# The tiles that epilogues read are requested on GpSimd's queue instead of SyncE's

## The chip, the cores and the metric

The kernel runs on one core of a Trainium2 chip. The metric is device time in microseconds (us), the time of one execution of the whole program. Five engines work side by side, each through its own list of instructions in order: TensorE (PE in the profile; PEld is its weight load), VectorE (DVE), ScalarE (ACT), GpSimd (POOL) and SyncE (SP), which here only issues transfers. A transfer is asked for by an instruction in the list of one of these engines ("a queue" below) and then runs on the core's 16 DMA engines. An engine that has to wait for a semaphore holds back everything behind that instruction in its own list.

## The reference

One layer of a hybrid decoder over 2,048 tokens (16 meta tokens ahead of them) of width 1,024, in float32. Cut to what matters here:

```python
u = rmsnorm(hres, norm_w)
proj = einsum('bld,dn->bln', u, w_in)          # inputs of both branches, and the merge gates
z, xbc, dt_raw, q, k, v, g_gla, a_lr, merge_g = split_cols(proj, IN_WIDTHS)
y_ssd, y_gla = ...                             # the two branches (Mamba-2 SSD, gated linear attention)
branches = stack([y_ssd, y_gla], axis=2)
branch_proj = einsum('blnc,ncd->blnd', branches, w_branch)
gates = sigmoid(merge_g.reshape(b, l, 2, 1024))
merged = sum(gates * branch_proj, axis=2)
h = hres + einsum('bld,de->ble', merged, w_out)
return rmsnorm(h, final_norm_w)[:, 16:]
```

Five matrix products of 2,048 x 1,024 x 1,024 are done in the part of the kernel that the change touches: the two merge gates, the two branch projections and the output projection.

## The kernel before

The kernel has two parts. The first (up to some 1,486 us) does the input projection and both branches; the change does not touch it. The second part does the five products named above, each split over two halves of the tokens where the stage is a gate or a branch. Its stages run one after the other: gate0, br00, br10 (first half of the tokens), gate1, br01, br11 (second half), out. Names in the trace: `g` are the gates in DRAM, `m` the merged rows, `out_h` the result, `in_xm` the residual rows, `in_w_br`, `in_w_o` and `in_w_feat` weights.

**Products.** Each stage multiplies blocks by a Strassen-like scheme with seven products in place of eight. A pair n has seven products p = 1 to 7; a product is 12 matmuls (four slices, three passes L211, L212, L213, since each float32 operand is split into a high and a low part) into a PSUM bank of 128 x 512. Products go in groups of 14, two pairs n and n+1 interleaved, in the order p = 1, 2, 6, 7, 5, 3, 4, each p first for n and then for n+1. There are 280 products in all; gate stages have 56, branch stages 28 each, the out stage 56. Three PSUM pools serve them: `psa` (three banks; p = 1, 6, 5 add into one bank, and p = 3 adds to it again), `psc` (p = 2) and `psb` (p = 7, 4). After p = 1, 6 and 5 ScalarE copies the bank to SBUF (`sn`, L1097, a snapshot), and p = 3 may add to the bank only when the snapshot that follows p = 5 has been taken.

**Operands.** For each product, SP loads the raw tiles: `load_b` (L1051, `br`, 256 KB, 28 for a stage, from a pool of five buffers and another of two) and `load_a` (L1063, `ar`, 256 KB, eight for each two pairs, from a pool of eight). ScalarE rounds the raw tile (L1056 for b, L1080 for a), VectorE makes the remainder (L1057, L1081); VectorE also adds a-tiles (L1071 to L1074).

**Epilogues.** A finished result is used by `use`. Gate stages take tanh on ScalarE (L1116) and store to `g`. Branch stages read the gate tile back (`fetch`, L1129, into an `io` buffer), multiply it with the result on VectorE (L1135), and the merged tile is stored to `m` for the first branch (L1031) and added into `m` by an accumulating transfer for the second (L1034). The out stage reads residual rows (`fetch`, L1152), adds half the snapshot and half the result (L1157, L1166), takes the sum of squares on ScalarE (L1172), raises it to the power -0.5 on GpSimd (L1182, a tile of 128 x 1), scales (L1187) and stores (L1031). All of these tiles come from one pool of eight `io` buffers; a buffer is free again when the store of what it held has landed.

**What sets the order.** The lists of PE and SP are in the order in which the program writes them: positions in units of a product, such as "three products ahead of its use" for a `fetch`, and "4.8 products ahead of its preparation" for a b-tile. Stores are issued on GpSimd. The lists of DVE, ACT and POOL are put in order by a scheduler from its own estimate of when each instruction becomes ready.

Each request of a queue reports its landing on one of eight counters, which are handed out in turn; a request therefore waits until the one eight places ahead of it in its own list has landed.

Of the kernel before, what the change touches and what calls it, by code (L numbers as in the profile page):

```python
# [14 lines left out]
P = 128  # L15
D = 1024
KT = 8
META = 16
BLK = 512
# [22 lines left out]
def trunk_kernel(ctx: ExitStack, tc: tile.TileContext, xm, xmt, w_feat, w_tok, w_zm, w_br, w_o,  # L42
                 cf32, cmsk, pvec, fnw, hvec, gw2, out):
    nc = tc.nc
# [20 lines left out]
    def left(name):  # L65
        return wdram.tile([P, BLK], F32, tag=name, name=name, bufs=1)
# [52 lines left out]
    for s in range(nsb):  # L119
        b = 2 * s + 2  # L120
# [898 lines left out]
    g_left = [[left(f"g_{b}_{i}") for i in range(16)] for b in range(nblk)]  # L1019
# [83 lines left out]
    def io():  # L1103
        return mk(opl, [P, BLK], F32, "io", bufs=8)

    def total(ps, snap):
        if snap is None:
            return ps
        nc.vector.tensor_tensor(snap, snap, ps, op=ALU.add)
        return snap  # L1110
# [12 lines left out]
    def branch_stage(s, nb):  # L1123
        got = {}

        def fetch(n, i, t):
            d, b = 2 * n + i, 2 * s + t
            got[n, i, t] = io()
            nc.sync.dma_start(got[n, i, t], g_left[b][nb * 8 + d])  # L1129

        def use(n, i, t, ps, snap):
            d, b = 2 * n + i, 2 * s + t
            th = got.pop((n, i, t))
            x = total(ps, snap)
            nc.vector.scalar_tensor_tensor(th, th, 1.0, x, op0=ALU.add, op1=ALU.mult)  # L1135
            if nb == 0:
                store(m_left[b][d // 4][:, d % 4], th)
            else:
                added.setdefault(step_no[0] + 2, []).append((m_left[b][d // 4][:, d % 4], th))

        return Stage(f"br{nb}{s}", ("b", nb, s), 4,
                     lambda n, i, j: w_br[nb * 8 + 2 * n + i, :, j * BLK:(j + 1) * BLK].rearrange(
                         "p (k c) -> p k c", c=P), use, fetch, 3)

    def out_stage():
# [3 lines left out]
        def fetch(n, i, t):  # L1149
            r0 = (2 * n + i) * P  # L1150
            res[n, i, t] = r = io()
            nc.sync.dma_start(r, xm[META + r0:META + r0 + P, t * BLK:(t + 1) * BLK])  # L1152

        def before(n, i, t, snap):
            r = res[n, i, t]
# [8 lines left out]
        def finish(row, n, i, t, ps):  # L1164
# [18 lines left out]
            for hf in (1 - t, t):  # L1183
# [11 lines left out]
                else:  # L1195
# [3 lines left out]
        return Stage("out", ("o",), seq // (2 * P),  # L1199
                     lambda n, i, j: m_left[(2 * n + i) // 4][j][:, :, (2 * n + i) % 4 * P:((2 * n + i) % 4 + 1) * P],  # L1200
                     use, fetch, 3, before)

    stages = []
# [150 lines left out]
```

## Time and profile before

| what | value |
|---|---|
| median of three runs | 2272.17 us (2272.05 to 2272.39) |
| the profiled execution | 2275.24 us, span 2273.5 us |
| mean granted clock of TensorE | 0.995 |
| busy share of the span: PE, DVE, ACT, POOL | 98%, 72%, 49%, 22% |
| `L1129` requests on SP (gate tiles) | 64 of 256 KB, 1635.2 to 2095.7 us |
| `L1152` requests on SP (residual rows) | 32 of 256 KB, 2098.5 to 2238.5 us |
| `L1031` and `L1034` requests on POOL | 184 of 256 KB, 1511.0 to 2232.7 us |

The profiled execution is 3.07 us longer than the median, and 1.74 us of it lie outside the span. Times in the views are microseconds from the start of the span. A row of the timeline gives start, length, engine, line, operation, the tile written and the tile read, and in square brackets the idle time of the engine just before and what ended it. In the table of stretches the columns are the stretch and its length, then busy time and number of instructions of PE, PEld, DVE, ACT and POOL, the granted clock, the DMA engines' share and GB/s. The second part takes the span from 1,486 us to its end; the br11 stage begins its products near 2,022 us and the out stage near 2,101 us.

### The profile page before, as it was taken

The page shows a single profiled execution, that of the slowest core. Times are in us where ns is not written, and L with a number is a line of the kernel's source. Part 1 is how long each engine was busy: PE and PEld are TensorE (multiplying, and loading weights), DVE is VectorE, ACT ScalarE, POOL GpSimd, SP SyncE. Part 2 cuts the span into 40 slices and gives each one's busy share as a digit, 9 for nine tenths or more (in the row PEclk, how much of TensorE's full clock was granted, in tenths as well). Part 3 has the DMA queues.
Part 4 walks back from the last instruction along what each step waited for, and adds up shares of the span by engine and source line. Part 5 has one row for each costly group of instructions (what it writes and reads, how often), then busy time and mean ns, then how long its engine had stood idle before and what let it go on. Part 6 is the DMA issues. An engine that isn't in the chain of part 4 may idle for free.

```text
span 2273.5 us, 36613 instructions
## 1 busy us (share of the span) xinstructions
PE 2232.8 (98%) x12699; PEld 1950.6 (86%) x12699; DVE 1629.2 (72%) x3323; ACT 1123.6 (49%) x2510; POOL 499.0 (22%) x633
## 2 busy tenths in 40 slices
PE   9899999999999999999999999999999999999998
PEld 9899888888888989888988898878888888887786
DVE  5787866687775578676579755785778866787876
ACT  5555555454444454443455343464644545554443
POOL 3344533122321222222122200012111122111211
PEclk9999999999999999999999999999999999999999
DMA  8767865667886666886576655475769865779653
GB/s 267 236 212 242 299 219 205 215 189 236 268 281 201 202 224 209 272 275 222 186 229 218 222 182 167 151 239 183 264 217 288 244 210 198 273 269 242 195 165 111
DMA packets 282377, 507.50 MB, mean 223 GB/s; under 512 B 27104, under 2 KB 134880, under 8 KB 282192
## 3 DMA queue, kind: packets, MB, share of 16 engines
q1 hardware_dynamic: 218096, 415.33, 55.7%
q0 software_dynamic: 16928, 48.77, 7.0%
q10 hardware_dynamic: 47168, 41.07, 5.5%
q8 instruction: 99, 1.62, 0.3%
q14 instruction: 86, 0.70, 0.1%
HBM read 357.87 MB, written 147.19 MB: 222 GB/s over the span
## 4 chain that ended last, share of the span: by engine, by line
PE 72%; DVE 9%; issue 9%; DMA 5%; ACT 3%; POOL 2%; SPq 1%; ACTq 0%; POOLq 0%; DVEq 0%
PE pj L211 13%; PE pj L213 13%; PE pj L212 13%; PE psa L211 4%; PE psa L213 4%; PE psa L212 4%; PE psb L213 2%; PE psb L211 2%; PE psb L212 2%; PE pc L653 2%; PE pc L823 2%; PE pc L654 1%; PE pc L923 1%; PE psc L213 1%; PE psc L211 1%
## 5 line engine op out<-in xcount | busy, mean ns | idle before, releaser
L211 PE MATMUL pj<-u,whl 128*128 128x512 f32 (+1 forms) x1184 | 445.9, 377 | 9.6 <-ACT acc L563 5.2
L213 PE MATMUL pj<-u,whl 128*128 128x512 f32 (+1 forms) x1184 | 429.9, 363 | 0.0
L212 PE MATMUL pj<-u,whl 128*128 128x512 f32 (+1 forms) x1184 | 429.1, 362 | 0.0
L211 PE MATMUL pj<-whl,u 128*128 128x256 f32 (+1 forms) x992 | 288.3, 291 | 0.9 <-DMA whl<-k_zm 0.5
L213 PE MATMUL pj<-whl,u 128*128 128x256 f32 (+1 forms) x992 | 281.5, 284 | 0.6 <-DVE u L284 0.6
L212 PE MATMUL pj<-whl,u 128*128 128x256 f32 (+1 forms) x992 | 281.4, 284 | 0.0
L211 PEld LDWEIGHTS pj<-u,whl 128*128 128x128 f32 x1184 | 224.0, 189 | 47.6 <-ACT acc L563 6.2
L211 PE MATMUL psa<-b,a 128*128 128x512 f32 x640 | 250.0, 391 | 5.1 <-ACT sn L1097 5.1
L213 PEld LDWEIGHTS pj<-u,whl 128*128 128x128 f32 x1184 | 223.7, 189 | 35.6
L212 PEld LDWEIGHTS pj<-u,whl 128*128 128x128 f32 x1184 | 224.3, 189 | 33.0
L213 PE MATMUL psa<-b,a 128*128 128x512 f32 x640 | 249.3, 389 | 0.7 <-DVE a L1081 0.7
L212 PE MATMUL psa<-b,a 128*128 128x512 f32 x640 | 249.0, 389 | 0.0
L211 PEld LDWEIGHTS pj<-whl,u 128*128 128x128 f32 x992 | 189.3, 191 | 2.9 <-DMA whl<-k_zm 1.4
L213 PEld LDWEIGHTS pj<-whl,u 128*128 128x128 f32 x992 | 189.2, 191 | 1.0 <-DVE u L284 1.0
L212 PEld LDWEIGHTS pj<-whl,u 128*128 128x128 f32 x992 | 189.3, 191 | 0.4
L193 POOL TENSOR_TENSOR whl<-wr,whl 128x512 fp32r<-128x512 f32 (+1 forms) x96 | 135.8, 1423 | 170.3 <-ACT whl L190 134.3
L567 DVE SCALAR_TENSOR_TENSOR acc<-cin,hcw,acc 128x512 f32<-128x512 f32 (+1 forms) x192 | 160.1, 834 | 15.0 <-ACT acc L563 12.8
L1081 DVE TENSOR_TENSOR a<-ar,a 128x512 fp32r<-128x512 f32 x160 | 110.1, 688 | 78.2 <-ACT a L1080 77.6
L85 POOL TENSOR_TENSOR wr<-wr 128x256 f32<-128x256 f32 x80 | 68.8, 860 | 418.1 <-DMA wr<-u 163.1
L1056 ACT ACTIVATE b<-br 128x512 fp32r<-128x512 f32 x196 | 118.2, 626 | 62.4 <-DMA br<-br_t 24.0
L211 PEld LDWEIGHTS psa<-b,a 128*128 128x128 f32 x640 | 120.1, 188 | 33.0 <-ACT sn L1097 8.2
L213 PEld LDWEIGHTS psa<-b,a 128*128 128x128 f32 x640 | 120.1, 188 | 26.4 <-DVE a L1081 1.4
(307 smaller groups left out, 4866.7 us busy)
## 6 DMA issues: line engine op xcount, KB each, us to landing
whl<-k_s SPq DMA_DIRECT2D x96, 512.0 KB, 4.2
whl<-k_g SPq DMA_DIRECT2D x96, 512.0 KB, 4.3
whl<-k_v SPq DMA_DIRECT2D x48, 512.0 KB, 3.7
whl<-k_z SPq DMA_DIRECT2D x36, 512.0 KB, 4.3
wr<-in_w_feat SPq DMA_DIRECT2D x64, 256.0 KB, 4.5
k_s<-whl SPq DMA_DIRECT2D x32, 512.0 KB, 3.7
cb<-cumd ACTq DMA_DIRECT2D x64, 256.0 KB, 5.6
k_g<-whl SPq DMA_DIRECT2D x32, 512.0 KB, 3.8
```

Of the source, the lines that this page charges most:

```text
L85: (nc.vector if store is None else nc.gpsimd).tensor_tensor(o, x, y, op=ALU.subtract)
L193: (nc.gpsimd if low is None else nc.vector).tensor_tensor(hl[:, 1], raw, hl[:, 0].bitcast(F32), op=ALU.subtract)
L211: nc.tensor.matmul(ps, sh, mh, start=first, stop=False, **kw)
L212: nc.tensor.matmul(ps, sh, ml, start=False, stop=False, **kw)
L213: nc.tensor.matmul(ps, sl, mh, start=False, stop=last, **kw)
L567: nc.vector.scalar_tensor_tensor(acc, cin[:, k:k + tt], hcw[:, ti, k:k + 1], acc, op0=ALU.mult, op1=ALU.add)
L653: nc.tensor.matmul(py[:, h * 64:(h + 1) * 64], dm[:, h], xdt[:, h], start=True, stop=True)
L654: nc.tensor.matmul(py[:, 256:512], cf[:, a:a + P], s_ssd[:, g], start=True, stop=True)
L823: nc.tensor.matmul(ps[:, r * P:(r + 1) * P], kq[:, 2 * r * P:(2 * r + 1) * P], kq[:, (2 * r + 1) * P:(2 * r + 2) * P], start=True, stop=True)
L923: nc.tensor.matmul(po[:, :256], qg[:, c * P:(c + 1) * P], s_gla[:, h], start=False, stop=True)
L1056: nc.scalar.activation(t[:, 0], raw, AF.Copy)
L1081: nc.vector.tensor_tensor(t[:, 1], src, t[:, 0].bitcast(F32), op=ALU.subtract)
```

## The change

Two lines: the gate tile of a branch stage and the residual row of the out stage are requested on GpSimd's queue (`nc.gpsimd.dma_start`) rather than SP's.

```diff
@@ branch_stage, fetch
             d, b = 2 * n + i, 2 * s + t
             got[n, i, t] = io()
-            nc.sync.dma_start(got[n, i, t], g_left[b][nb * 8 + d])
+            nc.gpsimd.dma_start(got[n, i, t], g_left[b][nb * 8 + d])
@@ out_stage, fetch
             r0 = (2 * n + i) * P
             res[n, i, t] = r = io()
-            nc.sync.dma_start(r, xm[META + r0:META + r0 + P, t * BLK:(t + 1) * BLK])
+            nc.gpsimd.dma_start(r, xm[META + r0:META + r0 + P, t * BLK:(t + 1) * BLK])
```

SP's list goes from 1,316 rows to 1,220 and GpSimd's from 633 to 729: 96 requests move. The list of PE is the same. The lists of DVE and ACT hold the same instructions, in another order at some places.

Where br11 goes over into the out stage, SP's list loses two gate tiles among the loads of the out stage's first b-tiles (`br_4087` is the last tile of p = 7, `br_4089` and `br_4092` the first two of p = 5):

```order
 L1063 DMA ar_4078_23008<-m_0_0_17332 128x4x128
 L1063 DMA ar_4080_23026<-m_0_1_17333 128x4x128
-L1129 DMA io_4084_23035<-g_2_13_17313 128x512
 L1051 DMA br_4087_23043<-out_t0_3_216 128x512
 L1051 DMA br_4089_23062<-out_t0_0_213 128x512
-L1129 DMA io_4090_23064<-g_2_15_17315 128x512
 L1051 DMA br_4092_23069<-out_t0_1_214 128x512
```

The loads keep their order among each other.

At the same place, on ScalarE, the preparations of b-tiles (L1056) change their places against the two snapshots (L1097) that p = 3 waits for: `sn_4067` is that of pair n, `sn_4079` that of pair n+1 of br11's last group.

```order
 L1056 ACTIVATE b7_4099_23116<-br_4066_22967 128x512
+L1056 ACTIVATE b7_4102_23139<-br_4074_22999 128x512
 L1080 ACTIVATE a_4085_23037<-ar_4057_22935 128x512
-L1056 ACTIVATE b7_4102_23139<-br_4074_22999 128x512
+L1056 ACTIVATE b7_4106_23160<-br_4087_23043 128x512
 L1097 ACTIVATE sn_4067_22981<-psa_4024_22769 128x512
 L1080 ACTIVATE a_4091_23066<-ar_4076_23004 128x512
-L1056 ACTIVATE b7_4106_23160<-br_4087_23043 128x512
+L1056 ACTIVATE b5_4111_23172<-br_4089_23062 128x512
+L1056 ACTIVATE b5_4115_23195<-br_4092_23069 128x512
 L1097 ACTIVATE sn_4079_23022<-psa_4029_22792 128x512
```

The last preparation of p = 7 now stands ahead of the first snapshot, and the first two of p = 5 ahead of the second. The same exchange, with other numbers, stands at three more borders of stages: br00 to br10, br10 to gate1 and br01 to br11.

On GpSimd, in the out stage between its first and its second group, the list was, before,

```order
L1182 TENSOR_TENSOR ssf_4118_23214<-ssf_4118_23214,mhalf_62 128x1
L1031 DMA out_h<-io_4100_23134 128x512
L1031 DMA out_h<-io_4147_23341 128x512
L1182 TENSOR_TENSOR ssf_4124_23240<-ssf_4124_23240,mhalf_62 128x1
L1031 DMA out_h<-io_4108_23165 128x512
L1031 DMA out_h<-io_4159_23382 128x512
L1182 TENSOR_TENSOR ssf_4152_23366<-ssf_4152_23366,mhalf_62 128x1
L1182 TENSOR_TENSOR ssf_4167_23413<-ssf_4167_23413,mhalf_62 128x1
```

and with the change, from the last accumulating transfer of br11 on, it is

```order
L1034 DMA m_2_1_17337<-io_4090_23064 128x512
L1152 DMA io_4159_23382<-in_xm 128x512
L1152 DMA io_4160_23384<-in_xm 128x512
L1182 TENSOR_TENSOR ssf_4118_23214<-ssf_4118_23214,mhalf_62 128x1
L1031 DMA out_h<-io_4100_23134 128x512
L1031 DMA out_h<-io_4147_23341 128x512
L1152 DMA io_4184_23528<-in_xm 128x512
L1182 TENSOR_TENSOR ssf_4124_23240<-ssf_4124_23240,mhalf_62 128x1
L1152 DMA io_4188_23550<-in_xm 128x512
L1182 TENSOR_TENSOR ssf_4152_23366<-ssf_4152_23366,mhalf_62 128x1
L1031 DMA out_h<-io_4108_23165 128x512
L1031 DMA out_h<-io_4159_23382 128x512
```

The requests for the next group's residual rows stand between the powers and the stores of the group before; each waits there for the store of the buffer that it fills.

## The prediction

> **What bounds the kernel now.** I read the busy shares first, then what TensorE waited for in the second part, then TensorE's rows around each wait, and last the rows of SP, ACT, DVE and POOL that end it.
>
> ```profile
> PE 2232.8 (98%) x12699; PEld 1950.6 (86%) x12699; DVE 1629.2 (72%) x3323; ACT 1123.6 (49%) x2510; POOL 499.0 (22%) x633
> PE psa L211 <- ACT sn L1097: 5.1, 5, 2.4
> ```
>
> TensorE sets the end: it is busy 98% of the span, and its list is not changed. So the change can only move what TensorE waits. The second row (engine, line, what it waited for: us in total, times, longest) says that in the second part nearly all of this is p = 3 waiting for a snapshot on ScalarE, five times.
>
> ```profile
> 2098.72 0.39 PE L213 MATMUL psa<-b,a 128*128 128x512 f32 x1
> 2100.87 0.50 PE L211 MATMUL psa<-b,a 128*128 128x512 f32 x1 [1.76 <-ACT sn L1097]
> ...
> 2138.86 0.39 PE L213 MATMUL psa<-b,a 128*128 128x512 f32 x1
> 2141.63 0.50 PE L211 MATMUL psa<-b,a 128*128 128x512 f32 x1 [2.38 <-ACT sn L1097]
> ...
> 2179.62 0.39 PE L213 MATMUL psa<-b,a 128*128 128x512 f32 x1
> 2180.05 0.50 PE L211 MATMUL psa<-b,a 128*128 128x512 f32 x1
> ...
> 2218.03 0.39 PE L213 MATMUL psa<-b,a 128*128 128x512 f32 x1
> 2218.57 0.50 PE L211 MATMUL psa<-b,a 128*128 128x512 f32 x1 [0.15 <-ACT sn L1097]
> ```
>
> Undisturbed matmuls start 0.23 us apart here, and one after a wait lasts 0.11 longer (0.50 for 0.39). A stall is therefore the step between two starts less 0.23 plus 0.11: 2.03 us at the border from br11 to the out stage, then 2.65, 0.31 and 0.42 in the first three groups of the out stage. Together 5.4 us, or 0.24% of the kernel: more cannot be won. The fifth wait, at the start of br01, is ended by loads ahead of which the change removes nothing, and I leave it.
>
> **The border from br11 to the out stage.** SP asks for operands and gate tiles in one list, and a request waits there until the one eight places ahead has landed.
>
> ```profile
> 2085.41 2.12 SPq L1129 DMA_DIRECT2D io<-g  x1
> 2087.80 0.32 SPq L1051 DMA_DIRECT2D br<-out_t  x1
> ...
> 2093.05 1.61 SPq L1129 DMA_DIRECT2D io<-g  x1
> 2094.71 0.90 SPq L1051 DMA_DIRECT2D br<-out_t  x2
> ```
>
> ```profile
> L1129 SPq DMA_DIRECT2D io<-g x64: 319/382/2125, 1635.2 to 2095.7; - x64
> ```
>
> ```profile
> 2099.70 0.63 ACT L1056 ACTIVATE b<-br 128x512 fp32r<-128x512 f32 x1 [3.16 <-DMA br<-out_t]
> 2100.24 0.58 ACT L1097 ACTIVATE sn<-psa 128x512 f32<-128x512 f32 x1
> ...
> 2102.20 1.30 ACT L1056 ACTIVATE b<-br 128x512 fp32r<-128x512 f32 x2 [0.34 <-DMA br<-out_t]
> ```
>
> The first load at 2094.71 (the last b-tile of p = 7) lands 4.99 us later, at 2099.70, where ScalarE prepares it; only then comes the snapshot that TensorE has been waiting for, which ends at 2100.82. Up to the load at 2094.71 the gate tiles take 2.39 at 2085.41 (up to the next row), 1.66 at 2093.05, and 0.38 for one more just ahead of them (the median over all 64, min/median/max in ns, in the last row): 4.4 us. But some of that is waiting for a place, or for a `br` buffer, and passes on to the load behind. I take three quarters, 3.4 us earlier.
>
> ScalarE's new order takes back part. The preparation of 2099.70 now stands ahead of the first snapshot, that of pair n, needed for p = 3 of n:
>
> ```profile
> 2096.13 0.44 PE L211 MATMUL psa<-b,a 128*128 128x512 f32 x1
> ```
>
> That product starts at 2096.13, and needs its snapshot by 2096.08 (2100.82 and 2100.87 above are 0.05 apart). With the new order the snapshot ends 1.12 after the start of the preparation, at 2100.82 if the load comes no earlier, 4.74 too late. With 3.4 us gained, p = 3 of n stalls 1.3. Pair n+1's snapshot stands behind the second tile of p = 5, prepared at 2102.20: 2103.32 less 3.4 is 2099.9, and after a stall of 1.3 it is needed at 2100.1, so nothing is added. The border goes from 2.03 to 1.3: **-0.7** (bounds: -1.7 with all 4.4 us, +2.7 with none).
>
> **Three borders that had no stall** (br00 to br10, br10 to gate1, br01 to br11) get the same exchange on ScalarE.
>
> ```profile
> 1709.73 0.33 SPq L1129 DMA_DIRECT2D io<-g  x1
> 1710.51 0.98 SPq L1051 DMA_DIRECT2D br<-br_t  x2
> ```
>
> ```profile
> 1715.92 0.63 ACT L1056 ACTIVATE b<-br 128x512 fp32r<-128x512 f32 x1 [2.42 <-DMA br<-br_t]
> ...
> 1791.76 0.64 ACT L1056 ACTIVATE b<-br 128x512 fp32r<-128x512 f32 x1 [2.39 <-DMA br<-gate_t]
> ...
> 2020.36 0.63 ACT L1056 ACTIVATE b<-br 128x512 fp32r<-128x512 f32 x1 [1.79 <-DMA br<-br_t]
> ```
>
> ```profile
> 1714.61 0.39 PE L211 MATMUL psa<-b,a 128*128 128x512 f32 x1
> ...
> 1790.77 0.39 PE L211 MATMUL psa<-b,a 128*128 128x512 f32 x1
> ...
> 2019.97 0.39 PE L211 MATMUL psa<-b,a 128*128 128x512 f32 x1
> ```
>
> The second fence has the last preparation of p = 7 at each border, the third the start of p = 3 of n. Now the snapshot ends 1.12 after that preparation starts, and is needed 0.05 before the product: the load has to land 2.48, 2.16 and 1.56 us earlier, or TensorE stalls for the rest. Four gate tiles stand among the 16 requests ahead of that load. One costs between its own 0.38 (the median) and the 0.78 from 1709.73 to the next row; four at 0.58 are 2.3, three quarters of it 1.7. That leaves stalls of 0.8, 0.5 and 0: **+1.2** (bounds: 0 if all of the 4 x 0.78 = 3.1 arrive, +6.2 if nothing).
>
> **The first group of the out stage** (2.65).
>
> ```profile
> 2124.21 2.43 SPq L1152 DMA_DIRECT2D io<-in_xm  x2
> 2126.74 7.69 SPq L1063 DMA_DIRECT2D ar<-m  x4
> ```
>
> ```profile
> 2126.57 0.69 DVE L1071 TENSOR_TENSOR as<-ar,ar 128x512 f32<-128x512 f32 x1 [4.54 <-DMA ar<-m]
> ...
> 2131.39 0.69 DVE L1157 SCALAR_TENSOR_TENSOR io<-sn,io 128x512 f32<-128x512 f32 x1
> ...
> 2137.11 0.69 DVE L1071 TENSOR_TENSOR as<-ar,ar 128x512 f32<-128x512 f32 x1 [2.03 <-DMA ar<-m]
> ...
> 2139.65 0.68 DVE L1166 SCALAR_TENSOR_TENSOR io<-sn,io 128x512 f32<-128x512 f32 x1
> ```
>
> The snapshot is late because ScalarE waits for VectorE's L1166 at 2139.65, which stands behind the a-sums of 2137.11, and these waited 2.03 us for the last of the loads issued from 2126.74 on. Those stand behind the residual rows at 2124.21, which wait for buffers. Without the rows SP goes straight on to the four loads, and the sums of 2126.57 come earlier too: the load that they waited 4.54 us for stands behind other residual rows. VectorE cannot follow all the way: the last residual row must still be used at 2131.39, and its buffer comes free when the accumulating store has landed.
>
> ```profile
> 2119.98 0.86 POOL L1034 DMA_DIRECT2D m<-io  x1 [2.14 <-DVE io L1135]
> DMA to landing us min/median/max: 3.8/5.2/7.9
> ```
>
> ```profile
> io<-in_xm SPq DMA_DIRECT2D x32, 256.0 KB, 4.1
> ```
>
> The first fence is that last store with the landings of its kind (median 5.2 us), the second the landing of a residual row (4.1 us). The request went out at 2126.3 at the latest (the end of the pair at 2124.21 is 2126.64, less the 0.33 of one), so its buffer was free by then; 2126.3 + 4.1 is 2130.4, and the use at 2131.39 can come about 1.0 earlier. I take the middle between that 1.0 and the whole 2.65: **-1.8** (bounds: -2.65, and +1.7 if the store lands in 7.9 instead of 5.2 us and the row goes out 2.7 later).
>
> **The second and third group** (0.31 and 0.42).
>
> ```profile
> SPq L1152 <- DMA out_h<-io: 66.5, 22, 14.6
> ```
>
> SP stood 66.5 us at 22 residual rows until a store of the result had landed, with the next group's a-loads behind it. These go out as soon as their own buffers are free, which clears both stalls: **-0.7**.
>
> **What the moved requests cost on POOL.** The nearest rows are its own plain stores of the same 256 KB, here, and the accumulating store at 2119.98 above.
>
> ```profile
> L1031 POOL DMA_DIRECT2D m<-io x32: 542/542/556, 1660.0 to 2041.4; - x32
> 1641.00:1946.00 305.00, 304.98 (x1345) 252.17 (x1344) 224.85 (x373) 156.74 (x276) 50.81 (x80) 1.00 0.74 238
> ```
>
> 96 requests at 0.54 to 0.86 are 52 to 83 us (I take 0.54: a plain copy). POOL is busy 50.81 of 305 us from br00 to the end of gate1, so idle time hides it: nothing in the sum. If POOL is held at a request, the powers (L1182) and stores behind it are late, and with them VectorE's L1187 and the next `io` buffer; that is the second rival. After the last group no request stands ahead of the final powers, so the tail stays.
>
> A rule of the Trainium skill speaks here ("DMA: Bandwidth & Descriptors", section "SWDGE vs HWDGE vs iDMA"): GpSimd writes descriptors for its transfers into SBUF, where VectorE in a fast mode can lock it out. In this trace VectorE is busy 72% and POOL's 32 stores stay within 542 to 556 ns, so the rows show no such lock, and it would change no term.
>
> **Sum.** -0.7 + 1.2 - 1.8 - 0.7 = -2.0 us: 2275.24 becomes 2273.2 for a profiled execution, and against the median, which is 3.07 lower, 2272.17 becomes **2270.2**.
>
> **Rivals.**
>
> *All stalls go.* The loads gain the full time at every border, and the residual rows come early: -5.4, or **2266.8**. For it: idle time on POOL. Against it: ScalarE's new order needs 4.74 us at one border, more than the 4.4 that SP gives.
>
> *Only the issue time is saved.* If the landings set SP's pace, each tile taken away gives its own 0.38 and no more: 1.5 us at the three borders (stalls 1.0, 0.7, 0.1: +1.8) and 1.1 at the fourth (stall 3.6 for 2.03: +1.6). With the out stage's -2.5 this is +0.9, **2273.1**. The same time results if POOL, held at landings, takes back the out stage's gain. For it: the DMA engines are 74% busy over the first stretch above. Against it: 2.12 and 1.61 us at single gate tiles. The Trainium skill has this as a rule (the same page, "Issuing engines are not separate DMA queues": asking from another engine saves only the sequencer's time to ask).
>
> *The snapshots stand behind b-tiles that come no earlier: slower.* Place: the four borders. If what holds the b-loads is the `br` buffer, which VectorE frees, and not the gate tiles, the new order alone decides: 2.48 + 2.16 + 1.56, and 2.71 at the fourth, +8.9; less the 2.5 of the out stage, +6.4: **2278.6**. It decides from the point where the loads gain under 2.5 us at the first border and 4.7 at the fourth, and outweighs the out stage once they gain less than about 1.2 on the mean. For it: the wait for such buffers is SP's second largest,
>
> ```profile
> SPq L1051 <- DVE b L1057: 160.8, 71, 16.7
> ```
>
> though against it the loads at 1710.51 and 2094.71 came right behind a gate tile.
>
> **How the numbers follow.** Forecast 0.45, all stalls go 0.15, issue time only 0.22, slower 0.18. Some 0.2% (4.5 us) is what can be told from no change: under 2267.6 is faster, over 2276.7 slower. All stalls go counts as faster, with 0.03 of the forecast: 0.18. Slower gets 0.15 of its own case (the rest falls short of 4.5) and 0.01 from a longer hold on POOL: 0.16. Within 0.2%: 0.66. The range goes from 2266.6 (the first rival) to 2277.0, where the slower case begins; the forecast's own, with its terms at half their bounds, is 2267.5 to 2273.
>
> **What would show it.** SP's list without the 66.5 us; TensorE's wait for L1097 at the out stage's border near 1.3 and ahead of p = 3 of n instead of n+1; new waits of some 0.8 and 0.5 near 1714 and 1790, none near 2020; the out stage's first group under 1 us; `io` requests on POOL near 0.54 us. I am wrong if TensorE waits for something else than L1097, above all for VectorE or `psc` in the out stage, or if the new waits at the three borders exceed 2 us.

## The result, and the profile after

The change makes the kernel slower: 2293.17 us median of four runs (2291.88 to 2294.75) against 2272.11 for the kernel before (2272.03 to 2272.39), 21 us more. The ratio is 1.0095, with a 95% interval of 1.0083 to 1.0107. The profiled execution took 2292.2 us, its span is 2290.4, so 16.9 more than the span before.

Busy shares first, then what TensorE waited for in the second part, of the changed kernel:

```profile
PE 2237.6 (98%) x12699; PEld 1954.0 (85%) x12699; DVE 1624.8 (71%) x3323; ACT 1125.0 (49%) x2510; POOL 553.2 (24%) x729
PE psa L211 <- ACT sn L1097: 17.3, 9, 4.8
```

GpSimd is busy 54 us more, about what 96 requests of 0.55 us make; this lies in its idle time. The wait of p = 3 for a snapshot went from 5.1 us in five places to 17.3 in nine. In the table below a loss is counted from the last matmul ahead of a wait to the fourth undisturbed step behind it, less 0.227 us (the undisturbed step) for each matmul; these sums come from TensorE's rows of the profiled executions.

| lost at | before | changed |
|---|---|---|
| br00 to br10 | 0 | 1.9 |
| br10 to gate1 | 0 | 2.1 + 0.8 |
| br01 to br11 | 0 | 2.9 + 0.8 |
| br11 to out | 2.1 | 7.7 |
| out stage, first, second, third group | 2.7, 0.3, 0.5 | 1.0, 6.1, 1.0 |
| elsewhere, from 1,510 us on | 1.6 | 0.3 |

The borders cost 14.0 us more, the out stage 4.7, and 1.3 come back elsewhere: 17.4, against 16.9 in the span.

**The border to the out stage.** TensorE's rows, and two stretches behind the wait (columns as in the table of stretches before):

```profile
2102.51 0.39 PE L213 MATMUL psa<-b,a 128*128 128x512 f32 x1
...
2107.69 0.79 PE L211 MATMUL psa<-b,a 128*128 128x512 f32 x1 [4.80 <-ACT sn L1097]
2108.28 0.63 PE L212 MATMUL psa<-b,a 128*128 128x512 f32 x1
2108.71 0.63 PE L213 MATMUL psa<-b,a 128*128 128x512 f32 x1
```

```profile
2107.60:2113.40 5.80, 5.71 (x14) 4.48 (x15) 5.80 (x11) 4.05 (x9) 0.00 (x0) 0.51 0.93 330
2113.40:2119.20 5.80, 5.80 (x27) 4.79 (x26) 5.80 (x10) 3.83 (x7) 1.85 (x3) 1.00 0.86 176
```

The wait is 4.95 us of missing matmuls, and then the granted clock is 0.51 for 5.8 us: 14 matmuls where the next stretch has 27, at steps of 0.43. That adds 2.6 us to the loss (5.8 less 14 times 0.227). ScalarE, SP and VectorE at the same place:

```profile
2106.52 0.63 ACT L1056 ACTIVATE b<-br 128x512 fp32r<-128x512 f32 x1 [5.00 <-DMA br<-out_t]
2107.06 0.58 ACT L1097 ACTIVATE sn<-psa 128x512 f32<-128x512 f32 x1
```

```profile
2091.29 11.49 SPq L1063 DMA_DIRECT2D ar<-m  x4
2102.83 2.51 SPq L1051 DMA_DIRECT2D br<-out_t  x5
```

```profile
2093.20 0.69 DVE L1081 TENSOR_TENSOR a<-ar,a 128x512 fp32r<-128x512 f32 x1 [0.22 <-ACT a L1080]
...
2099.61 0.69 DVE L1071 TENSOR_TENSOR as<-ar,ar 128x512 f32<-128x512 f32 x1 [5.12 <-DMA ar<-m]
...
2101.55 0.68 DVE L1081 TENSOR_TENSOR a<-ar,a 128x512 fp32r<-128x512 f32 x1
```

The snapshot of pair n stands behind the last tile of p = 7, as the order said. That tile is asked for at 2102.83, just after TensorE should have started p = 3 (2102.51 + 0.23 = 2102.74). Before, the request went out 1.42 us ahead of that start (2094.71 against 2096.13); now it is 0.09 behind it. So SP, with no gate tiles left in its list, asks for this tile 1.5 us later, not earlier. Four a-loads ahead of it took 11.49 us, since each needs an a-buffer. The last of them reuses the buffer that VectorE's L1081 at 2101.55 gives free. In VectorE's new order that L1081 stands behind the a-sums of the next stage (- is its place before, + the places with the change):

```
 L1057 TENSOR_TENSOR b6_4093_23071<-br_4054_22928,b6_4093_23071 128x512
+L1071 TENSOR_TENSOR as_4069_22987<-ar_4059_22939,ar_4068_22985 128x512
+L1072 TENSOR_TENSOR as_4070_22988<-as_4069_22987,ar_4057_22935 128x512
+L1073 TENSOR_TENSOR ar_4059_22939<-ar_4057_22935,ar_4059_22939 128x512
 L1081 TENSOR_TENSOR a_4073_22996<-ar_4007_22670,a_4073_22996 128x512
-L1071 TENSOR_TENSOR as_4069_22987<-ar_4059_22939,ar_4068_22985 128x512
```

`ar_4080`, the last a-load, takes the buffer of `ar_4007`, which `a_4073` is made from. The sum `as_4069` waits for `ar_4068` to land, 5.12 us. In the kernel before the L1081 came first:

```profile
2088.84 0.69 DVE L1081 TENSOR_TENSOR a<-ar,a 128x512 fp32r<-128x512 f32 x1 [0.94 <-ACT a L1080]
2093.54 0.69 DVE L1071 TENSOR_TENSOR as<-ar,ar 128x512 f32<-128x512 f32 x1 [4.01 <-DMA ar<-m]
```

So two new orders work on each other: VectorE waits for a landing ahead of freeing a buffer, SP waits for that buffer ahead of a b-tile, and ScalarE waits for that b-tile ahead of a snapshot. The same exchange of L1071 and L1081 stands at the other three borders. Over the second part (from 1,520 us on), SP's wait for L1081 in the kernel before, and then in the changed one:

```profile
SPq L1063 <- DVE a L1081: 165.7, 43, 13.2
```

```profile
SPq L1063 <- DVE a L1081: 292.0, 67, 16.4
```

The wait is 126 us longer. SP no longer spends some 37 us on 96 requests (0.38 each) nor 66.5 us behind residual rows, and stands here longer instead.

**The second group of the out stage.** GpSimd, VectorE, ScalarE and TensorE of the changed kernel:

```profile
2174.57 0.54 POOL L1152 DMA_DIRECT2D io<-in_xm  x1 [2.81 <-DMA out_h<-io]
2175.11 1.21 POOL L1031 DMA_DIRECT2D out_h<-io  x2
2179.37 1.08 POOL L1152 DMA_DIRECT2D io<-in_xm  x2 [3.05 <-DMA out_h<-io]
```

```profile
2178.25 0.69 DVE L1157 SCALAR_TENSOR_TENSOR io<-sn,io 128x512 f32<-128x512 f32 x1 [4.69 <-DMA io<-in_xm]
...
2183.59 0.69 DVE L1157 SCALAR_TENSOR_TENSOR io<-sn,io 128x512 f32<-128x512 f32 x1 [4.05 <-DMA io<-in_xm]
...
2190.17 0.69 DVE L1071 TENSOR_TENSOR as<-ar,ar 128x512 f32<-128x512 f32 x1 [2.88 <-DMA ar<-m]
```

```profile
2193.48 0.63 ACT L1172 ACTIVATE junk<-io 128x512 bf16<-128x512 f32 x1 [7.22 <-DVE io L1166]
```

```profile
2194.74 0.50 PE L211 MATMUL psa<-b,a 128*128 128x512 f32 x1 [4.20 <-ACT sn L1097]
```

A request for a residual row waits for the landing of a store that GpSimd itself issued shortly before (2.81, 3.05 us), and the next two stores wait behind it: the pair at 2175.11 is issued after a request had waited, and the rows at 2179.37 wait for that pair in turn. When SP asked for the rows, such a wait held back loads, not the stores that it was waiting for. VectorE then stands 4.69 and 4.05 us at L1157. Behind these stands an L1081 (2185.41) that frees an a-buffer. The a-load into that buffer lands 3.93 us after it, the a-sum of 2190.17 waits for that load, and L1166 stands behind the sums. So L1166 is late for ScalarE, and the snapshot behind that is late for TensorE. The a-buffers are in this chain as well.

What the requests themselves cost is as forecast:

```profile
L1129 POOL DMA_DIRECT2D io<-g x64: 546/553/587, 1642.4 to 2090.2; - x64
DMA to landing us min/median/max: 2.9/4.6/9.0
```

### The profile page after: what moved, and what is told of

It reads as the page before. It is cut to its first block, busy times and chain, and to the rows that moved or that the text cites. A ratio compares the mean times of both kernels' runs of the same rounds, so it can differ in the third digit from the quotient of the medians.

```text
span 2290.4 us, 36567 instructions
## 1 busy us (share of the span) xinstructions
PE 2237.6 (98%) x12699; PEld 1954.0 (85%) x12699; DVE 1624.8 (71%) x3323; ACT 1125.0 (49%) x2510; POOL 553.2 (24%) x729
## 3 DMA queue, kind: packets, MB, share of 16 engines
q0 software_dynamic: 24608, 73.94, 10.6%
## 4 chain that ended last, share of the span: by engine, by line
PE 76%; DVE 8%; DMA 6%; issue 3%; ACT 3%; POOL 2%; SPq 1%; ACTq 0%; POOLq 0%; DVEq 0%
PE pj L211 13%; PE pj L213 13%; PE pj L212 13%; PE psa L211 5%; PE psa L213 5%; PE psa L212 5%; PE psb L211 2%; PE psb L212 2%; PE psb L213 2%; PE pc L653 2%; PE pc L823 2%; PE psc L212 1%; PE psc L213 1%; PE psc L211 1%; PE pc L654 1%
## 5 line engine op out<-in xcount | busy, mean ns | idle before, releaser
L211 PE MATMUL psa<-b,a 128*128 128x512 f32 x640 | 252.3, 394 | 17.3 <-ACT sn L1097 17.3
L1081 DVE TENSOR_TENSOR a<-ar,a 128x512 fp32r<-128x512 f32 x160 | 109.8, 686 | 76.3 <-ACT a L1080 75.7
L1056 ACT ACTIVATE b<-br 128x512 fp32r<-128x512 f32 x196 | 118.1, 626 | 59.6 <-DMA br<-br_t 30.0
```

What stands on the lines that cost most here:

```text
L211: nc.tensor.matmul(ps, sh, mh, start=first, stop=False, **kw)
L1056: nc.scalar.activation(t[:, 0], raw, AF.Copy)
L1081: nc.vector.tensor_tensor(t[:, 1], src, t[:, 0].bitcast(F32), op=ALU.subtract)
```

## The experiments

Theory A: the loss is made at the borders, by the orders shown above and by SP's a-loads, and in the out stage, by requests behind young stores in one list. Rivals were that it is one of the two places alone (B), that GpSimd's requests cost in themselves (B again, in act_io10) or take the DMA engines from the b-tiles (C), that the b-tiles' own buffers hold them (D), and others named with their runs. Medians were taken in sets, each beside the kernel before on the same chip; that kernel's median was 2269.7 to 2271.4 in these sets, so ratios are given and compared.

**One part of the change alone.** The gate tiles on GpSimd, the residual rows on SP:

```diff
-            nc.sync.dma_start(got[n, i, t], g_left[b][nb * 8 + d])
+            nc.gpsimd.dma_start(got[n, i, t], g_left[b][nb * 8 + d])
```

> Only the gate tiles of the branch stages (L1129) are requested on GpSimd; the residual rows stay on SP. Theory A (at the borders of stages ScalarE's new order puts the snapshots behind b-tiles, and these come hardly earlier because SP, freed of the gate tiles, stops at the a-loads that wait for their own buffers): the four border stalls of the changed kernel stay (1.9, 2.8, 3.6 and 5.1 us, with some 2 us of slower matmuls behind the last) and the out stage is as before: 13 to 15 us over before, 2285 to 2287 us. Rival B (the loss comes from GpSimd's list in the out stage, and the borders are its echo): within 2 us of before, 2270 to 2274 us.

Measured: 2283.22 us, ratio 1.0057 (1.0036 to 1.0078), 12 us over before and 2 under what was expected. Lost at the borders 1.7, 5.2, 4.1 and 8.0 us, in the out stage 1.4. The residual rows on GpSimd, the gate tiles on SP:

```diff
-            nc.sync.dma_start(r, xm[META + r0:META + r0 + P, t * BLK:(t + 1) * BLK])
+            nc.gpsimd.dma_start(r, xm[META + r0:META + r0 + P, t * BLK:(t + 1) * BLK])
```

> Only the residual rows of the out stage (L1152) are requested on GpSimd; the gate tiles stay on SP. Theory A: no new stall at the first three borders, some 2 us at the fourth as before, and in the out stage the residual rows come late for VectorE's L1157 in the second group (a stall of 4 to 5 us there) while the first group's 2.65 us shrinks to 1: 3 to 6 us over before, 2275 to 2278 us. Rival B: nearly the whole loss, 15 us or more over before.

Measured: 2278.78 us, 1.0043 (1.0027 to 1.0059), 8 us over before and just over what was expected. No loss at the first three borders, 5.3 at the fourth, 1.5, 7.3 and 0.7 in the out stage. VectorE's wait for residual rows in the two kernels, first out_only's, then the changed one's:

```profile
DVE io L1157 <- DMA io<-in_xm: 9.6, 3, 4.1
```

```profile
DVE io L1157 <- DMA io<-in_xm: 21.4, 6, 4.7
```

12 and 8 make the 21 us nearly whole, and B falls in both its forms: neither part alone makes the loss. Place by place the two do not add up so well: the borders lose 19 us with the gate tiles alone, some 3 more than in the changed kernel. And the fourth border loses 5.3 us with the residual rows alone, with ScalarE's order nearly the old one, which was not expected. Some 1.6 of that are matmuls at half rate behind a wait of 2.71 us; the wait before was 1.92 us and had none. Why the waits are longer there is left open.

**ScalarE's order.** The list of ScalarE in the second part as the program writes it, in the changed kernel and in the kernel before:

```diff
-    with tc.manual_schedule(engines={mybir.EngineType.PE, mybir.EngineType.SP}):
+    with tc.manual_schedule(engines={mybir.EngineType.PE, mybir.EngineType.SP, mybir.EngineType.Activation}):
```

> The changed kernel, with ScalarE's list of the second part in the order in which the program writes it too (snapshots right behind their products, ahead of the border's b-tiles of p = 7 and 5); what SP and TensorE do is the same, VectorE's and GpSimd's lists are ordered anew around it. Theory A: the four border stalls go, what is left is the out stage: 2276 to 2280 us. Rival C (the b-tiles land late in themselves because GpSimd's requests take the DMA engines from them, so TensorE would only wait for the b-tiles instead of the snapshots): the stalls stay in another form, 2288 us or more.

> The kernel before, with ScalarE's list of the second part as the program writes it; all requests stay where they were. Theory A: the border's stall of 2.03 us goes and nothing else of size: 2268 to 2272 us, and so at least 5 us faster than the changed kernel with the same order. Rival C: the difference between the two queues stays near 21 us, whatever ScalarE's order.

Measured: 2281.37 us (1.0053, 1.0036 to 1.0069) with the change, 2272.52 (1.0012, 1.0002 to 1.0022) without, just over the 2268 to 2272 expected. The first three borders lose nothing in either, the fourth 1.3 us with the change: with the snapshots ahead of the b-tiles the stalls go, though the b-tiles are no earlier (at the first border the tile is asked for at 1712.89, some 3.5 us behind the start of p = 3). So C falls for the borders. The first snapshot at the border from br00 to br10 now waits only for TensorE:

```profile
1709.53 0.60 ACT L1097 ACTIVATE sn<-psa 128x512 f32<-128x512 f32 x1 [1.08 <-PE psa L213]
```

The time was above the 2276 to 2280 expected with the change, since the written order has its own loss of 11.5 us in the out stage's first group, where VectorE waits 7.1 us for one residual row (and 4.2 near 1826 us). Without the change that place loses 4.1 and 0.6. So the late residual row is there with either order of ScalarE, in another group.

**The b-tiles ahead of the a-loads.** In both kernels:

```diff
-                at(pos - (4.8 if si else 0.1), lambda st=st, p=p, j=j: st.load_b(p, j))
+                at(pos - (5.9 if si else 0.1), lambda st=st, p=p, j=j: st.load_b(p, j))
```

> The changed kernel, with the b-tiles of a new stage asked for 5.9 instead of 4.8 products ahead of their preparation. In SP's list the last tile of p = 7 then stands ahead of the three a-loads that wait for buffers, and the first tile of p = 5 ahead of the fourth; ScalarE's order at the borders is as in the changed kernel. Theory A (what holds the b-tiles is the a-loads in front of them): the waits of p = 3 of pair n at the four borders (1.9, 2.1, 2.9, 5.1 us, and the slow matmuls behind the last) go, some of those of n+1 stay: 2278 to 2283 us. Rival D (the buffers of the b-tiles hold them, or the DMA engines): SP only waits at the b-loads instead, and the time stays within 3 us of the changed kernel's 2293.

> The kernel before with the same 5.9 instead of 4.8. ScalarE's order at the borders then becomes much like that of the changed kernel. Theory A: with the tile of p = 7 early, that order costs nothing, and the border's 2.06 us goes: 2268 to 2272 us. Rival D: the new order costs 8 us or more, as it would with loads that come no earlier: 2278 us or more.

Measured: 2287.94 us (1.0074, 1.0057 to 1.0091) and 2274.02 (1.0021, 1.0010 to 1.0031). Both missed. At the borders the expected did happen: none, 2.4, none and 2.8 us lost in the changed kernel. But the borders from a gate to a branch stage, which lose nothing in the changed kernel, lose 1.2 and 3.7 us, and the out stage 15.5 in the profiled execution, which was the slowest of the four (2294.74). The kernel before, with ScalarE's order now much like that of the changed kernel, loses nothing at the first three borders, 2.5 at the fourth, 1.7 and 3.5 at the borders from a gate to a branch stage and 4.7 in the out stage. With b-loads earlier the a-loads behind them are later: the place in SP's list is worth as much as what stands there.

**More a-buffers.** SP's list unchanged, ScalarE's with the b-tiles ahead of the snapshots; to make room, two snapshot buffers fewer:

```diff
-    rpl = pool2("rawa", 8)
+    rpl = pool2("rawa", 10)
...
-                sn = mk(opl, [P, BLK], F32, "sn", bufs=6)
+                sn = mk(opl, [P, BLK], F32, "sn", bufs=4)
```

> The changed kernel with ten instead of eight a-load buffers, and four instead of six snapshot buffers to make room. SP's list is the same and ScalarE's has the last tile of p = 7 ahead of the first snapshot as in the changed kernel (one more tile of p = 5 stands ahead of the second). Theory A (at the borders SP stops at a-loads that wait for a buffer, and that holds the b-tiles behind them): SP's wait of L1063 for VectorE's L1081 falls clearly under the 292 us, the last tile of p = 7 is asked for 2 us or more earlier, and the stalls at the four borders (1.9, 2.8, 3.6, 7.7 us) fall under half: 2278 to 2285 us. Rival D (the b-tiles' own buffers or the DMA engines hold them): the borders stay and so does the time, 2288 to 2294 us.

Measured: 2273.90 us, 1.0006 (0.9997 to 1.0016): the loss of the change can no longer be told from none, which is better than expected. SP's wait, and its rows at the border to the out stage:

```profile
SPq L1063 <- DVE a L1081: 144.7, 46, 16.3
```

```profile
2084.26 5.79 SPq L1063 DMA_DIRECT2D ar<-m  x4
2090.14 5.55 SPq L1051 DMA_DIRECT2D br<-out_t  x5
```

The four a-loads take 5.79 us, not 11.49, and the last tile of p = 7 is asked for 3.7 us ahead of p = 3 (2093.62 + 0.23, less 2090.14) in place of 0.1 behind. The borders lose 0, 1.6, 0.2 and 6.9 us, the out stage nothing: residual rows are still waited for (12.6 us), but with a-tiles early VectorE has that to spare. D falls for the first three borders: the b-tiles' buffers are the same. Only the border to the out stage keeps its loss. There the tile took 6.5 us to land (2090.14 to its preparation at 2096.64), in a stretch in which the DMA engines are busy throughout (a share of 1.01). They were so in the kernel before too (1.07 from 2094.7 to 2099.7, and the tile landed in 4.99 us), so how much of the fourth border's loss is the load on the DMA engines, and not SP's list, no run here separates.

Two controls. Four snapshot buffers and nothing else:

> The changed kernel with four instead of six snapshot buffers and nothing else; ScalarE's order at the borders is that of the changed kernel. It is the control for the two runs that made room for other buffers so. Theory A: the four border stalls stay (together 10 to 17 us) and the out stage's too: 2288 to 2296 us. Rival F (fewer snapshot buffers were what helped, by holding ScalarE back): under 2284 us.

Measured: 2288.97 us, 1.0077 (1.0060 to 1.0095), with 1.3, 4.1, 3.8 and 6.0 us at the borders and 8.6 in the out stage. So it is not the snapshot buffers. And the kernel before with ten a-buffers:

> The kernel before with ten a-load and four snapshot buffers; every engine's list stays word for word. Theory A: SP is held by buffers of a-loads here too, so the border's 2.06 us shrinks, and the out stage's 2.67, 0.33 and 0.45 us may: 2266 to 2271 us, and the change of queues with ten buffers (2273.9) is then still a loss of 3 to 8 us. Rival G (with ten buffers the queues make no difference): 2272 to 2275 us.

Measured: 2270.48 us, 0.9997 (0.9988 to 1.0006). The kernel before gains nothing, and its interval overlaps that of the change with ten a-buffers: with these, whether the queues still differ is less than these runs can tell. In the profiled execution its out stage loses 0.1 us in place of 3.5, but the border to it 3.9, where a loss under 2.06 was expected. With the residual rows alone on GpSimd and ten a-buffers:

> Residual rows on GpSimd, gate tiles on SP, ten a-load and four snapshot buffers. Theory A: the first three borders as before (none), the border to the out stage 2 us or less, the out stage free of stalls as it was with both kinds on GpSimd and ten a-load buffers: 2265 to 2270 us. Rival G: 2272 to 2275 us.

Measured: 2271.68 us, 1.0005 (0.9995 to 1.0015), with 5.2 us lost at the border to the out stage, where 2 or less were expected: no gain either.

**More `io` buffers.** In both kernels:

```diff
-        return mk(opl, [P, BLK], F32, "io", bufs=8)
+        return mk(opl, [P, BLK], F32, "io", bufs=10)
...
-                sn = mk(opl, [P, BLK], F32, "sn", bufs=6)
+                sn = mk(opl, [P, BLK], F32, "sn", bufs=4)
...
-    late_sums = [make_sums(opl, "io", 8, *sums[key], j, c, None) for key in late for j in range(4) for c in range(2)]
+    late_sums = [make_sums(opl, "io", 10, *sums[key], j, c, None) for key in late for j in range(4) for c in range(2)]
```

> The changed kernel with ten instead of eight io buffers, and four instead of six snapshot buffers to make room. Theory A for the out stage (on GpSimd each request for a residual row waits for a store that was issued shortly before it in the same list, and the next store waits behind it): with two buffers more the wait is for an older store, VectorE's wait for residual rows (21.4 us in the changed kernel) falls under 8 and the second group's stall of 6.1 us under 2; the borders stay: 2284 to 2289 us. Rival E (the request is late because GpSimd's list places it late, not for want of a buffer): the second group's stall stays at 4 us or more, 2291 us or more.

> The kernel before with ten io and four snapshot buffers. Theory A: SP's 66.5 us of waiting for stores of the result shrinks, the out stage's stalls (2.67, 0.33, 0.45 us) fall under 1 us together, the border's 2.06 us stays: 2268.5 to 2271 us. Rival E: as before, 2272 us. Four snapshot buffers too few would show as ScalarE's snapshots waiting for VectorE, and more than 2272 us.

Measured: 2280.61 us (1.0045, 1.0030 to 1.0060), better than expected, and 2271.05 (0.9998, 0.9986 to 1.0009). In the changed kernel the out stage loses nothing any more, and the wait of L1157 for residual rows is gone from VectorE's list of waits; what it waits for now is its own inputs:

```profile
DVE io L1157 <- ACT sn L1097: 12.6, 10, 2.0
DVE io L1157 <- PE psb L213: 8.6, 8, 1.4
```

Against four snapshot buffers alone (1.0077) that is some 7 us. So E falls: GpSimd's list is much the same, and an older store is all it takes. The borders keep 1.3, 4.5, 4.1 and 8.9 us. The kernel before, with these buffers, keeps 1.8 us in the out stage's first group, more than the 1 expected. Residual rows alone on GpSimd with the same buffers:

> Residual rows on GpSimd, gate tiles on SP, ten io and four snapshot buffers. Theory A: no stall at the first three borders, and none of size in the out stage, where only a store that is older by two is waited for; the border to the out stage keeps 2 to 5 us: 2267 to 2272 us, 7 us or more under the same split with eight buffers (2278.8). Rival E: what eight buffers showed comes back, 2275 us or more.

Measured: 2273.85 us, 1.0010 (0.9999 to 1.0021); nothing lost in the out stage, 1.3 at the first border and 6.4 at the fourth. The time is above what was expected, by that border. Then ScalarE's list as written as well, for the residual rows alone, for both, and for neither on GpSimd:

> The same, with ScalarE's list of the second part as the program writes it. Theory A: the border to the out stage goes too, what is left are the two stalls of 0.6 and 0.9 us that the written order had in the branch and gate stages: 2265 to 2269 us, faster than both kernels. Rival: the written order has ScalarE wait for residual rows in the out stage as it did with eight buffers on both queues: 2272 us or more.

> The changed kernel (both kinds of tiles on GpSimd) with ten io and four snapshot buffers and ScalarE's list as written. Theory A: with both causes taken away, the snapshots behind b-tiles and the residual rows behind young stores, the change of queues costs nothing any more: what is left is the stall of 4.2 us of the written order near 1826 us: 2268 to 2274 us. Rival B: requests on GpSimd cost in themselves; 2278 us or more.

> The kernel before with ScalarE's list as written, ten io and four snapshot buffers: the control for the two runs that had these with the change. Theory A: the stall of 4.1 us near 2134 us goes, as buffers held it: 2267 to 2271 us, and the change with the same order and buffers (2278.4) costs 7 us or more by what its gate tiles do to the a-loads. Rival G: 2275 us or more, no difference of queues.

Measured: 2272.65 (1.0004, 0.9995 to 1.0013), 2278.42 (1.0029, 1.0019 to 1.0040) and 2273.09 (1.0009, 1.0000 to 1.0018). All three are above what was expected, and no version beats the kernel before. The first two times even lie where their rivals had them (2272 and 2278 us or more). With both tiles on GpSimd 6.2 us stay in the out stage's first group, 4.3 with neither. The chain that ends at that wait goes through an a-load that takes 7.27 us to land with the change, and through a residual row that takes 5.94 without; what makes them slow was not followed further. So in this order 0.2% remain for the change that theory A does not account for. Against B stand the requests themselves (0.55 us each, and a landing after 4.6 in the changed kernel) and ten a-buffers, with all 96 requests on GpSimd and a ratio of 1.0006.

**The sums out of VectorE's list.** The four a-sums of the first pair of each stage on GpSimd, alone and with ten `io` and four snapshot buffers:

```diff
-            nc.vector.tensor_tensor(s1, a21, a22, op=ALU.add)
+            (nc.gpsimd if n == 0 else nc.vector).tensor_tensor(s1, a21, a22, op=ALU.add)
...
```

> The changed kernel, with the four a-sums (L1071 to L1074) of the first pair of each stage on GpSimd instead of VectorE. SP's list is the same, ScalarE's still has the last tile of p = 7 ahead of the first snapshot. Theory H (what holds SP's a-loads at the borders is that VectorE, in its new order, has the first pair's sums, which wait for an a-tile to land, ahead of the L1081 that frees the buffer SP waits for): that L1081 comes 4 us or more earlier, SP gets through its four a-loads earlier by as much, and the border stalls (1.9, 2.1, 2.9, 5 us and what follows) fall under 1 us each; the out stage's stalls stay: 2278 to 2285 us. Rival D (the a-loads are held by TensorE's pace whatever VectorE's order): the borders stay, 2288 us or more.

> The same, with ten io and four snapshot buffers. Theory H together with the young stores of the out stage: neither cause is left, 2268 to 2275 us, within 3 us of the kernel before with both kinds of tiles still on GpSimd. Rival D: 2278 us or more, as with ten io buffers alone (2280.6).

Measured: 2292.25 us (1.0100, 1.0084 to 1.0116) and 2281.90 (1.0054, 1.0035 to 1.0073): both times missed, and lie where rival D had them. The mechanism that D denies shows all the same in the rows of SP and VectorE at the border to the out stage (sums_pool):

```profile
2090.84 7.71 SPq L1063 DMA_DIRECT2D ar<-m  x4
2098.60 3.22 SPq L1051 DMA_DIRECT2D br<-out_t  x5
```

```profile
2094.71 0.69 DVE L1081 TENSOR_TENSOR a<-ar,a 128x512 fp32r<-128x512 f32 x1 [0.94 <-ACT a L1080]
...
2102.03 1.74 DVE L1081 TENSOR_TENSOR a<-ar,a 128x512 fp32r<-128x512 f32 x1
```

The freeing L1081 comes at 2094.71, p = 3 being due at 2102.01 (7.3 ahead; 1.2 in the changed kernel), SP is through its a-loads in 7.71 us instead of 11.49, and the b-tile is asked for 3.4 ahead of p = 3. The borders lose 0, 1.3, 0.9 and 6.5 us for 1.9, 2.8, 3.6 and 7.7. But the sums on GpSimd cost elsewhere: 2.6 and 1.6 us near 1520, 2.0 near 1640 and 4.4 near 1950, the out stage loses 10.6 in place of 8.1, and while they ran here VectorE was slow, as the last row shows (1.74 us for an operation of 0.69). GpSimd's row:

```profile
2099.94 1.60 POOL L1071 TENSOR_TENSOR as<-ar,ar 128x512 f32<-128x512 f32 x1
```

So VectorE's order is shown to hold SP, and to make most of the loss of the first three borders (2.2 of 8.4 us are left) together with ScalarE's. That it is all of the fourth border's is not shown: 6.5 us are lost there though the tile is asked for earlier than in the kernel before.

## Why the prediction was wrong

The forecast was 2270.2 us in a range of 2266.6 to 2277.0; the time is 2293.17. What bounds the kernel was right, and so were the places: nearly all that is lost lies behind waits of TensorE for a snapshot, at the borders and in the out stage. The sum failed by its terms, and most of all by one that it did not have: the a-loads that stand in SP's list ahead of the b-tiles, and the a-buffers that they wait for. SP's rows of these loads in the kernel before, at the first border and at the border to the out stage:

```profile
1704.46 5.04 SPq L1063 DMA_DIRECT2D ar<-in_w_br  x4
```

```profile
2088.55 4.41 SPq L1063 DMA_DIRECT2D ar<-m  x4
```

The changed kernel at the first border, the a-loads, the load behind them and TensorE's last row ahead of p = 3:

```profile
1701.08 8.48 SPq L1063 DMA_DIRECT2D ar<-in_w_br  x4
1709.61 2.32 SPq L1051 DMA_DIRECT2D br<-br_t  x5
```

```profile
1713.35 0.39 PE L213 MATMUL psa<-b,a 128*128 128x512 f32 x1
```

- **Three borders, +1.2.** Measured +8.4 in the profiled execution (1.9, 2.9, 3.6). The step that failed is "three quarters" of the gate tiles' time as a gain of the load. SP did win time of that size: it comes to the four a-loads 12.5 us ahead of p = 3 (1713.35 + 0.23 less 1701.08) instead of 10.2 (1714.61 less 1704.46), and it is 2.7 and 2.1 us earlier at the next two borders. It lost the time again at the a-loads, 8.48 us for 5.04, since VectorE's L1081 gives their buffer free 5.1 us ahead of p = 3 (1708.52) instead of 7.3 (1707.32). At the first border the b-load is 4.0 us ahead of p = 3 (1713.58 less 1709.61) where it was 4.1, at the next two 3.1 where it was 4.4 and 2.8 where it was 5.0. I had put the part that is not gained down to a place in the queue or a `br` buffer, and bounded it from 0 to all; what happened is the nothing at the lower end, and less than nothing at two of the borders. With second waits of 0.8 us at these two, even the +6.2 was passed. The sign that I named for being wrong came too: the wait at the third of these borders is 2.74 us.
- **The border to the out stage, -0.7.** Measured +5.7. The bounds there ended at +2.7, with a load that gains nothing. SP comes to the a-loads 11.4 us ahead of p = 3 instead of 7.6, so it won 3.9 us, but the freeing L1081 stands 1.2 us ahead instead of 7.3, and the load lost 1.5 us. I showed ScalarE's order and did not follow VectorE's, though it decides when the buffers of SP's loads come free. The view that gave SP's second largest wait (160.8 us for `br` buffers) had the largest above it, these 165.7 us for a-buffers. The rest is the slow clock behind the wait, +2.6, that no term had. (Three quarters of 4.4 are 3.3, not 3.4; this changes nothing.)
- **The out stage, -1.8 and -0.7.** Measured -1.7 in the first group (2.7 to 1.0), and +5.8 and +0.6 in the second and third. The step that failed is that the a-loads "go out as soon as their own buffers are free, which clears both stalls". Their buffers come free behind L1157, which needs the residual rows, and these came later than before. The first group's number is as forecast, but partly by luck. By the chain of the kernel before, the a-load that the sums of 2137.11 waited for went out at 2133.91, right behind the L1081 of 2133.28 that freed its buffer, and not behind residual rows as I had it; the changed kernel's wait there ends by the same chain, from a residual row over L1157, L1081 and an a-load to L1166. The second rival named the hold of POOL at landings, but as taking back the gain, not as a loss of its own.
- **The waits left out.** I left the wait at the start of br01 as it was, and counted no other; the five waits for L1097 also include one of 0.39 us near 1526, while the step at 2180.05 is none of them. In the changed kernel's profiled execution both are gone, and they are most of the 1.3 us that come back elsewhere.
- **POOL, 0.** Right: requests cost 0.55 us, in idle time. What costs is what stands behind them.
- **The slower rival** was right at the borders that the snapshots stand behind b-tiles that come no earlier (the new order alone, +8.9 us; measured +14.0, of which 2.6 are the slow clock) but wrong on the holder, which is the a-loads' buffers, and took the out stage's -2.5 as given. Its chance of 0.18 and its price of 2278.6 were both too low.

The Trainium skill's rule named with the second rival ("DMA: Bandwidth & Descriptors", "Issuing engines are not separate DMA queues": another engine saves only the sequencer's time) has the trace on its side in that little was to be won: a tile's request took SP 0.38 us, and SP came 2.3 us earlier to the a-loads of the first border. It does not speak of the lists in which requests then stand.

## What to carry to other kernels

When requests leave a queue, look for what the queue stops at next: count the buffers of the loads that stay, and find the instruction that frees each. Where a scheduler orders engines from its own estimate, a change of transfers alone reorders them; follow the new order on every engine that is waited for, also on the one that only frees buffers. A request that waits for a store's landing does not belong into the list that issues the next stores, unless enough buffers make that store an old one.

## What the runs showed of the hardware

After some waits TensorE ran at half its rate: 0.51 of the clock for 5.8 us behind the wait of 4.95 us above, steps of 0.43 for 0.23 us, at a price of up to 3.0 us more than the wait itself (ar10_sn4, 6.9 us lost by a wait of 3.95). In the second part of all the runs each wait of more than 3.4 us was followed by such a stretch (the shortest 3.47, in branch_only; one of 3.37 in sums_pool_io10 was not). Of those between 2.0 and 3.4 some were and some not: the kernel before had 2.54 us at 2138.86 and full rate behind it,

```profile
2141.60:2147.40 5.80, 5.77 (x25) 4.80 (x26) 4.88 (x9) 3.10 (x7) 1.53 (x3) 1.00 0.01 3
```

while 2.06 us in sn4 cost 3.8. The Trainium skill ("TensorE: Matmul & The Clock Gate", Part 1) has such a gate, with windows of about 3.4 us that run freely and half the clock after an idle one; these rows agree for the long waits, and show that shorter ones can cost it too.

VectorE's operations on two tiles took 1.57 to 1.74 us instead of 0.69 while GpSimd added tiles at the border to the out stage in sums_pool (2100.5 to 2107.1), and were back at 0.68 after it. Requests on GpSimd landed no later than SP's by the median: 4.6 us for a gate tile, where SP's took 5.3.
